# Batched 64x64 matmul on one core: the first tile of a loaded as fp32 by SyncE and ScalarE

## The chip, the cores and the metric

The kernel runs on one core of a Trainium2 chip. The metric is the device time of one execution in microseconds. The core has TensorE (PE, which also loads weights, shown as PEld), VectorE (DVE), ScalarE (ACT), GpSimd (POOL) and SyncE (SP), and sixteen DMA engines, which all queues share. SyncE, ScalarE and GpSimd can each issue DMAs on a queue of their own.

## The reference

```python
a = np.random.randn(1024, 64, 64).astype(np.float32)
b = np.random.randn(1024, 64, 64).astype(np.float32)
np.matmul(a, b).astype(np.float32)
```

1024 independent products of 64x64 matrices: 16.78 MB of `a`, 16.78 MB of `b` and 16.78 MB of result.

## The kernel before

The work is cut into 16 tiles `t` of 64 products each. `b` is loaded by such tiles (`load_b`, 1.05 MB each); `a` is loaded by 8 double tiles `s` of 128 products (`load_a`, 2.1 MB of fp32 each), so that tiles 2s and 2s+1 use double tile s.

**Loads of a.** `load_a(s)` issues four DMAs from GpSimd, one for each quarter `h`, into a tile `a_sb`. They cast from fp32 to bf16 on the way, so they write half of what they read. `a_pool` holds three such tiles.

**Loads of b.** `load_b(t)` issues one DMA from SyncE, or from ScalarE for tiles 1, 4, 6 and 7. `b_pool` holds four tiles. The loads of tiles 0 and 1 carry a gate: they wait until the second quarter of the first tile of `a` has landed.

**Preparing a.** `regroup(s)` copies `a_sb` into `a_bf` with the four quarters interleaved; it is one VectorE copy, and for `s == 0` four, one for each quarter. `transpose(s, j)` runs eight TensorE transposes with an identity matrix, taking pairs of bf16 as one fp32, and ScalarE copies the result from PSUM into `at_sb`. `spread(t)` then makes four VectorE copies that put the quarters on the diagonal blocks of a block-diagonal tile `at_bd`. There are two `at_bd` tiles, used in turn; both are set to zero at the start, the first by VectorE, the second by GpSimd, and only the diagonal blocks are ever rewritten.

**Multiplying.** `cast(t)` makes bf16 of `b` on ScalarE. `multiply(t)` runs 64 matmuls (128x128 weights from `at_bd`, 64 columns of `b`) into two PSUM tiles `o_ps`. ScalarE empties the first half and VectorE the second, four copies each, into a result tile `o_sb`; `o_pool` holds six. `store(t)` sends `o_sb` to memory from GpSimd, one tile after it was made (`HOLD = 2`); the last two tiles are stored in smaller pieces.

**Order.** The kernel is written under a manual schedule: each engine runs its instructions in the order of the program text, so an engine that waits holds up all that stands behind it. Before the loop over `t` stand the loads of the first three tiles of `a` and four of `b`, `regroup(0)`, both transposes of tile 0, `spread(0)`, `cast(0)`, `regroup(1)` and half of the transposes of tile 1. In the loop, each turn does `spread(t + 1)` and `cast(t + 1)`, the load of tile t+4 of `b`, on even turns `regroup(s + 2)` and the load of tile s+4 of `a`, then `multiply(t)`, half a set of transposes, and the store of the tile before. So VectorE empties tile 0 only after `regroup(2)`, that is after the third tile of `a` has landed. Every DMA from GpSimd signals on one of eight slots used in turn, and waits until the DMA that used its slot before has landed.

At the very start stand 100 small matmuls on zeros, which keep TensorE active before the first real work.

Of the kernel before, what the change touches and what calls it, by code (L numbers as in the profile page):

```python
# [8 lines left out]
fp32 = mybir.dt.float32  # L9
bf16 = mybir.dt.bfloat16  # L10
# [3 lines left out]
def kernel(  # L14
# [14 lines left out]
    nc = tc.nc  # L29
    B, M, K = a.shape  # L30
    _, _, N = b.shape
# [8 lines left out]
    a_v = a.rearrange("(s g h) (mp v) k -> s h g mp (v k)", h=4, g=32, v=16)  # L40
    b_v = b.rearrange("(t g h) (kp u) n -> t (h kp) g (u n)", h=4, g=16, u=2)
    o_v = out.rearrange("(t gh x) (mo w) n -> t (x mo) gh (w n)", gh=8, x=8, w=4)

    consts = ctx.enter_context(tc.tile_pool(name="consts", bufs=1))
# [3 lines left out]
    o_pool = ctx.enter_context(tc.tile_pool(name="o_pool", bufs=6))  # L48
    t_psum = ctx.enter_context(
        tc.tile_pool(name="t_psum", bufs=4, space=bass.MemoryType.PSUM)  # L50
    )
# [4 lines left out]
    bd_tiles = [  # L56
        consts.tile([128, 2, 16, 2, 4, 16], fp32, name=f"at_bd{i}") for i in range(N_BD)
    ]
    identity = consts.tile([128, 128], fp32)
    warm = consts.tile([128, 2], fp32)  # L60
    zeros = consts.tile([128, 32], bf16)
    a_tiles, b_tiles, abf_tiles, at_tiles, bbf_tiles = {}, {}, {}, {}, {}
    held, first_a = {}, []

    def load_a(s):
        a_sb = a_pool.tile([128, 4, 16, 64], bf16, name="a_sb")
        for h in range(4):
            load = nc.gpsimd.dma_start(  # L68
                out=a_sb[:, h, :, :].rearrange("p v k -> p (v k)"), in_=a_v[s, h]
            )  # L70
            if s == 0:
                first_a.append(load)
        a_tiles[s] = a_sb

    def load_b(t):
        b_sb = b_pool.tile([128, 16, 128], fp32, name="b_sb")
        queue = nc.scalar if t in (1, 4, 6, 7) else nc.sync
        load = queue.dma_start(out=b_sb[:], in_=b_v[t])  # L78
        if t < 2:
            tc.add_manual_dep(  # L80
                load.ins,
                first_a[1].ins.name,
                mybir.DependencyInfo(
                    mybir.DependencyClass.Sync, mybir.DependencyReason.DATA
                ),
                reason="first tile of a goes ahead",
            )
        b_tiles[t] = b_sb

    def regroup(s):  # L90
        a_sb = a_tiles.pop(s)
        a_bf = work.tile([128, 16, 4, 64], bf16, name="a_bf")

        for lo, hi in [(0, 1), (1, 2), (2, 3), (3, 4)] if s == 0 else [(0, 4)]:
            nc.vector.tensor_copy(  # L95
                a_bf[:, :, lo:hi, :],
                a_sb[:, lo:hi, :, :].rearrange("p h v k -> p v h k"),
            )
        abf_tiles[s] = a_bf
        at_tiles[s] = work.tile([128, 2, 32, 2, 4, 4], fp32, name="at_sb")  # L100

    def transpose(s, j):
        a_cols = abf_tiles[s][:].rearrange("p v h k -> p v (h k)").bitcast(fp32)
        for wl in range(2):
            at_ps = t_psum.tile([128, 4, 128], fp32, name="at_ps")
            for vo in range(4):
                nc.tensor.transpose(  # L107
                    at_ps[:, vo, :], a_cols[:, 4 * vo + 2 * j + wl, :], identity[:]
                )
            nc.scalar.copy(  # L110
                at_tiles[s][:, j, :, wl, :, :],
                at_ps[:].rearrange("p vo (g mp) -> p g mp vo", mp=4),
            )

    def spread(t):
        half = slice(16 * (t % 2), 16 * (t % 2) + 16)
        bd = bd_tiles[t % N_BD]
        for h in range(4):
            rows = slice(32 * h, 32 * h + 32)
            nc.vector.tensor_copy(  # L120
                bd[rows, :, :, :, h, :].rearrange("p j g wl mo -> p j (g wl) mo"),
                at_tiles[t // 2][rows, :, half, :, :, :].rearrange(
                    "p j g wl mp vo -> p j (g wl) (mp vo)"
                ),
            )

    def cast(t):
        b_bf = work.tile([128, 16, 128], bf16, name="b_bf")
        b_sb = b_tiles.pop(t)
        if t < n_t - 1:  # L130
            nc.scalar.copy(b_bf[:], b_sb[:])  # L131
        else:
            for gq in range(4):
                rows = slice(4 * gq, 4 * gq + 4)
                if gq % 2:
                    nc.vector.tensor_copy(b_bf[:, rows, :], b_sb[:, rows, :])
                else:
                    nc.scalar.copy(b_bf[:, rows, :], b_sb[:, rows, :])  # L138
        bbf_tiles[t] = b_bf

    def store(t):
        for piece in held.pop(t):
            piece()
# [49 lines left out]
            held[t] = [lambda q=q: put(q, 8 if whole else 4) for q in ([0] if whole else [0, 4])]  # L193

    with tc.manual_schedule():
        load_a(0)

        warm_ps = t_psum.tile([128, 4, 128], fp32, name="at_ps")
        nc.vector.memset(zeros[:], 0.0)
        for _ in range(100):  # L200
            nc.tensor.matmul(  # L201
                warm_ps[0:32, 0, 0:32], zeros[:], zeros[:], start=True, stop=True
            )

        nc.vector.memset(warm[:, 0:1], 0.0)  # L205
        nc.scalar.copy(warm[:, 1:2], warm[:, 0:1])  # L206
        for t in range(B_AHEAD):
            load_b(t)
        nc.vector.memset(bd_tiles[0][:], 0.0)  # L209
        make_identity(nc, identity)  # L210
        for s in range(1, A_AHEAD):
            load_a(s)
        nc.gpsimd.memset(bd_tiles[1][:], 0.0)  # L213
        regroup(0)
        transpose(0, 0)
        transpose(0, 1)
        spread(0)
        cast(0)
        regroup(1)
        load_a(A_AHEAD)  # L220
        transpose(1, 0)
        for t in range(n_t):
            s, half = t // 2, t % 2
            if t + 1 < n_t:
                spread(t + 1)
                cast(t + 1)
            if t + B_AHEAD < n_t:
                load_b(t + B_AHEAD)
            if half == 0:
                if s + 2 < n_s:  # L230
                    regroup(s + 2)
                if s + 1 + A_AHEAD < n_s:
                    load_a(s + 1 + A_AHEAD)
            multiply(t)
            if half == 0 and s + 1 < n_s:
                transpose(s + 1, 1)
            if half == 1 and s + 2 < n_s:
                transpose(s + 2, 0)
            if t >= HOLD - 1:
                store(t - HOLD + 1)  # L240
        for t in range(n_t - HOLD + 1, n_t):
            store(t)
# [30 lines left out]
```

## Time and profile before

| What | Value |
|---|---|
| Median of 9 runs | 135.89 us (135.55 to 136.08) |
| The profiled execution | 135.76 us, span 133.7 us |
| VectorE busy | 105.7 us, 79% of the span |
| ScalarE busy | 84.6 us, 63% |
| TensorE busy | 70.0 us, 52% |
| GpSimd busy | 44.4 us, 33% |
| HBM traffic | 33.55 MB read, 16.78 MB written |
| GpSimd's DMA queue | 25.17 MB written, 66.4% of the DMA engines' time |
| SyncE's DMA queue | 12.58 MB, 26.2% |
| ScalarE's DMA queue | 4.19 MB, 8.3% |

The span runs from the first to the last instruction in the profile; 2.06 us of the profiled execution lie outside it. Times below are microseconds from the start of the span. The DMA figures count written bytes, so a casting load of `a` shows half of the bytes that it reads. L68, for example, is line 68 of the kernel before: L68 is the issue of a load of `a`, L78 that of a load of `b`, L95 `regroup`, L107 and L110 the transposes and their copies, L120 `spread`, L131 to L138 `cast`, L153 the stores, L164 the emptying of PSUM, L176 the matmuls, L201 the matmuls on zeros, L209 and L213 the two memsets of `at_bd`.

### The profile page before, as it was taken

To read this page: it belongs to the slowest core of one execution; us is meant where nothing else is said; L and a number is where in the kernel's file an instruction comes from. 1 tells how busy PE (TensorE), PEld (TensorE's weight loads), DVE (VectorE), ACT (ScalarE), POOL (GpSimd) and SP (SyncE) were. 2 spreads that over 40 slices of the span, in tenths; PEclk is the share of its full clock that TensorE was granted. 3 is DMA by queue.
4 is the path that set the end of the run, shared out by engine and by line. 5 is a ranking of instruction groups with operands and counts; after the bars stand their busy time and mean duration, and the time that the engine had idled before them with its cause. 6 is when DMAs were issued, how large, how long until landed. Compare 5 with 4: busy or idle time off the path is not lost.

```text
span 133.7 us, 3019 instructions
## 1 busy us (share of the span) xinstructions
PE 70.0 (52%) x1252; PEld 65.7 (49%) x1252; DVE 105.7 (79%) x148; ACT 84.6 (63%) x123; POOL 44.4 (33%) x59
## 2 busy tenths in 40 slices
PE   7108205753991396439926963496349633668000
PEld 7008105743991395439915952485248522658000
DVE  5621559059899899998999999999999999999900
ACT  4003303996637999956699999659948939259300
POOL 6938634331512431225023251124031204042820
PEclk9955955586589658975797799769986998555955
DMA  2999999999999999999999999999999999999990
GB/s 13 189 200 259 307 306 287 273 283 310 307 278 274 352 361 284 302 332 389 393 338 267 289 390 392 317 269 300 398 396 393 395 398 395 394 404 406 385 347 34
DMA packets 17485, 42.14 MB, mean 315 GB/s; under 512 B 1088, under 2 KB 1088, under 8 KB 17472
## 3 DMA queue, kind: packets, MB, share of 16 engines
q0 software_dynamic: 9024, 25.17, 66.4%
q1 hardware_dynamic: 6336, 12.58, 26.2%
q10 hardware_dynamic: 2112, 4.19, 8.3%
q8 instruction: 10, 0.16, 0.5%
q14 instruction: 3, 0.02, 0.0%
HBM read 33.55 MB, written 16.78 MB: 376 GB/s over the span
## 4 chain that ended last, share of the span: by engine, by line
DMA 64%; DVE 14%; issue 12%; POOL 4%; POOLq 1%; DVEq 0%
DMA a_sb<-in_a_dram 50%; DMA out_dram<-o_sb 14%; DVE o_sb L164 8%; DVE at_bd L120 6%; POOL out_dram L153 3%; POOL a_sb L68 1%; POOLq L268 1%; DVE a_bf L95 0%; DVEq L95 0%; POOLq L153 0%; DVEq L120 0%; POOLq L257 0%
## 5 line engine op out<-in xcount | busy, mean ns | idle before, releaser
L176 PEld LDWEIGHTS <-at_bd 128*128 128x128 bf16 x1024 | 43.8, 114 | 42.7 <-DVE o_sb L164 25.5
L176 PE MATMUL o_ps<-b_bf,at_bd 128*128 128x64 bf16 x960 | 42.7, 215 | 37.7 <-DVE o_sb L164 23.4
L120 DVE COPY at_bd<-at_sb 32x1024 f32<-32x1024 f32 x64 | 46.5, 727 | 6.7 <-ACT at_sb L110 4.8
L164 DVE COPY o_sb<-o_ps 64x512 f32<-64x512 f32 x60 | 41.3, 688 | 2.1 <-PE o_ps L176 1.2
L164 ACT COPY o_sb<-o_ps 64x512 f32<-64x512 f32 x60 | 34.8, 580 | 6.8 <-PE o_ps L176 4.5
L131 ACT CAST b_bf<-b_sb 128x2048 bf16<-128x2048 f32 x15 | 28.6, 1905 | 13.8 <-DMA b_sb<-in_b_dram 13.8
L153 POOL DMA_DIRECT2D out_dram<-o_sb x20 | 20.1, 1005 | 48.7 <-DVE o_sb L164 17.1
L68 POOL DMA_DIRECT2D a_sb<-in_a_dram x32 | 20.3, 640 | 34.4 <-DMA a_sb<-in_a_dram 23.3
L107 PE MATMUL at_ps<-identity,a_bf 128*128 128x128 f32 x128 | 24.2, 354 | 13.4 <-DVE a_bf L95 13.4
L107 PEld LDWEIGHTS at_ps<-identity,a_bf 128*128 128x128 f32 x128 | 20.2, 187 | 13.7 <-issue 13.7
L110 ACT COPY at_sb<-at_ps 128x512 f32<-128x512 f32 x32 | 17.9, 588 | 10.3 <-PE at_ps L107 10.0
L95 DVE COPY a_bf<-a_sb 128x4096 bf16<-128x4096 bf16 (+1 forms) x11 | 10.3, 937 | 10.5 <-DMA a_sb<-in_a_dram 10.4
L176 PE MATMUL at_ps<-b_bf,at_bd 128*128 128x64 bf16 x64 | 3.5, 240 | 1.2 <-DVE at_bd L120 1.2
L209 DVE MEMSET at_bd<- 128x4096 f32 x1 | 3.5, 3472 | 0.8 <-issue 0.8
L213 POOL MEMSET at_bd<- 128x4096 f32 x1 | 3.5, 3530 | 0.0
L164 DVE COPY o_sb<-at_ps 64x256 f32<-64x256 f32 x8 | 3.4, 422 | 0.1
L138 ACT CAST b_bf<-b_sb 128x512 bf16<-128x512 f32 x2 | 1.1, 614 | 3.6 <-DMA b_sb<-in_b_dram 3.6
L201 PE MATMUL at_ps<-zeros 128*32 128x32 bf16 x100 | 2.8, 188 | 0.9 <-DVE warm L205 0.9
L201 PEld LDWEIGHTS <-zeros 128*32 128x32 bf16 x100 | 2.7, 103 | 0.9 <-DVE warm L205 0.9
L78 ACT MOVE_SHAPE b_sb<-in_b_dram x4 | 0.1, 24 | 4.8 <-DMA a_sb<-in_a_dram 4.8
L164 ACT COPY o_sb<-at_ps 64x256 f32<-64x256 f32 x8 | 2.9, 367 | 0.1
L206 ACT ACT_TABLE_LOAD x1 | 1.3, 1283 | 0.7 <-PEq L257 0.7
(10 smaller groups left out, 2.0 us busy)
## 6 DMA issues: line engine op xcount, KB each, us to landing
out_dram<-o_sb POOLq DMA_DIRECT2D x14, 1024.0 KB, 22.8
a_sb<-in_a_dram POOLq DMA_DIRECT2D x32, 256.0 KB, 18.5
out_dram<-o_sb POOLq DMA_DIRECT2D x2, 512.0 KB, 6.1
out_dram<-o_sb POOLq DMA_DIRECT2D x4, 256.0 KB, 5.5
b_sb<-in_b_dram SPq DMA_DIRECT2D x12, 0.5 KB, 21.7
b_sb<-in_b_dram ACTq DMA_DIRECT2D x4, 0.5 KB, 15.8
```

Of the source, the lines that this page charges most:

```text
L68: load = nc.gpsimd.dma_start(out=a_sb[:, h, :, :].rearrange("p v k -> p (v k)"), in_=a_v[s, h])
L95: nc.vector.tensor_copy(a_bf[:, :, lo:hi, :], a_sb[:, lo:hi, :, :].rearrange("p h v k -> p v h k"),)
L107: nc.tensor.transpose(at_ps[:, vo, :], a_cols[:, 4 * vo + 2 * j + wl, :], identity[:])
L110: nc.scalar.copy(at_tiles[s][:, j, :, wl, :, :], at_ps[:].rearrange("p vo (g mp) -> p g mp vo", mp=4),)
L120: nc.vector.tensor_copy(bd[rows, :, :, :, h, :].rearrange("p j g wl mo -> p j (g wl) mo"), at_tiles[t // 2][rows, :, half, :, :, :].rearrange(
L131: nc.scalar.copy(b_bf[:], b_sb[:])
L153: nc.gpsimd.dma_start(out=o_v[t, :, lo : lo + n, :], in_=o_sb[:, lo : lo + n].rearrange("p gh j wl n -> p (gh j wl n)"),)
L164: copy(dst, src)
L176: nc.tensor.matmul(o_ps[:, gl, g % 2, j, :], at_bd[:, j, g, :, u], b_bf[:, g, 64 * u : 64 * u + 64], start=(u == 0), stop=(u == 1),)
L201: nc.tensor.matmul(warm_ps[0:32, 0, 0:32], zeros[:], zeros[:], start=True, stop=True)
L209: nc.vector.memset(bd_tiles[0][:], 0.0)
L213: nc.gpsimd.memset(bd_tiles[1][:], 0.0)
```

## The change

Four things change, all in the opening of the kernel.

1. The first tile of `a` is loaded without a cast: quarters 0 and 2 by SyncE and 1 and 3 by ScalarE, as fp32, into two result buffers of `o_pool` that no result uses yet. These are the first instructions of both queues.
2. `regroup(0)` makes bf16 of the quarters while it interleaves them, quarters 0 and 2 on VectorE, 1 and 3 on ScalarE.
3. The loads of `b` lose their gate. They follow on the same queues, behind the quarters of `a`.
4. The 100 matmuls on zeros and the memset for them are gone. GpSimd, which has no load of tile 0 to issue, makes the identity matrix, zeroes the second `at_bd`, and then issues the loads of tiles 1 and 2 of `a`; before, this memset came after them.

```diff
+    def load_first_a():
+        raw = [
+            o_pool.tile([128, 8, 2, 2, 64], fp32, name="o_sb")[:].rearrange(
+                "p gh j wl n -> p (gh j wl n)"
+            )
+            for _ in range(2)
+        ]
+        parts = [raw[h % 2][:, 1024 * (h // 2) : 1024 * (h // 2) + 1024] for h in range(4)]
+        for h in range(4):
+            (nc.scalar if h % 2 else nc.sync).dma_start(out=parts[h], in_=a_v[0, h])
+        a_tiles[0] = parts
...
-        load = queue.dma_start(out=b_sb[:], in_=b_v[t])
-        if t < 2:
-            tc.add_manual_dep(
-                load.ins,
-                first_a[1].ins.name,
...
-                reason="first tile of a goes ahead",
-            )
+        queue.dma_start(out=b_sb[:], in_=b_v[t])
...
-        for lo, hi in [(0, 1), (1, 2), (2, 3), (3, 4)] if s == 0 else [(0, 4)]:
-            nc.vector.tensor_copy(
-                a_bf[:, :, lo:hi, :],
-                a_sb[:, lo:hi, :, :].rearrange("p h v k -> p v h k"),
-            )
+        if s == 0:
+            for h in range(4):
+                copy = nc.scalar.copy if h % 2 else nc.vector.tensor_copy
+                copy(a_bf[:, :, h, :], a_sb[h].rearrange("p (v k) -> p v k", v=16))
+        else:
+            nc.vector.tensor_copy(a_bf[:], a_sb[:].rearrange("p h v k -> p v h k"))
...
-        load_a(0)
-
-        warm_ps = t_psum.tile([128, 4, 128], fp32, name="at_ps")
-        nc.vector.memset(zeros[:], 0.0)
-        for _ in range(100):
-            nc.tensor.matmul(
-                warm_ps[0:32, 0, 0:32], zeros[:], zeros[:], start=True, stop=True
-            )
+        load_first_a()
...
         make_identity(nc, identity)
+        nc.gpsimd.memset(bd_tiles[1][:], 0.0)
         for s in range(1, A_AHEAD):
             load_a(s)
-        nc.gpsimd.memset(bd_tiles[1][:], 0.0)
         regroup(0)
```

## The prediction

> **What bounds the kernel now.** The first thing to read is the head of the page: the span, the DMA row of the slices, and the HBM traffic.
>
> ```profile
> span 133.7 us, 3019 instructions
> DVE  5621559059899899998999999999999999999900
> DMA  2999999999999999999999999999999999999990
> HBM read 33.55 MB, written 16.78 MB: 376 GB/s over the span
> ```
>
> The 16 DMA engines are busy from the second slice to the last but one, and VectorE (DVE) is nearly full from the tenth slice on. Two resources look like the bound, so the next question is which of them ends last. The DMA rate answers it. The GB/s column counts written bytes, and a load that casts `a` to bf16 reads twice what it writes. So I take the long middle stretch as one window, and five short ones at the start. Columns: busy us of PE, PEld, DVE, ACT, POOL with counts, then clock, DMA share, GB/s.
>
> ```profile
> 4.00:127.00 123.00, 67.15 (x1152) 63.00 (x1152) 103.36 (x146) 83.14 (x121) 40.88 (x49) 0.76 1.06 331
> 2.00:3.00 1.00, 1.00 (x45) 1.00 (x41) 1.00 (x1) 0.21 (x2) 1.00 (x2) 1.00 0.56 31
> 3.00:4.00 1.00, 0.77 (x30) 0.67 (x26) 1.00 (x1) 0.00 (x0) 0.93 (x4) 1.00 0.71 90
> 4.00:5.00 1.00, 0.00 (x0) 0.00 (x0) 1.00 (x1) 0.00 (x0) 1.00 (x3) 1.00 1.05 186
> 5.00:6.00 1.00, 0.00 (x0) 0.00 (x0) 0.47 (x2) 0.00 (x0) 1.00 (x3) 1.00 1.12 211
> ```
>
> From 4 to 127 us: 331 GB/s x 123 us = 40.7 MB written, and nearly all of the 8.4 MB that the casting loads read beyond what they write, so 49 MB in 123 us, or 0.398 MB per us. At 5 to 6 us, with only casting loads in flight, it is 2 x 211 KB, 0.42. The rate is nearly the same with loads of `a` alone, with a mix, and with stores alone (about 400 GB/s at 118 to 125 us). So the engines run at one ceiling from 4 us on, and the end is set by volume: 50.33 MB / 0.398 = 126.5 us after the moment at which they effectively start. That moment: 31 + 90 KB written by 4.0 us, 0.24 MB read, worth 0.6 us, so 4.0 - 0.6 = 3.4 us. 3.4 + 126.5 = 129.9 us; the last packet ends at 131.8 because the small last stores run slower (360 GB/s and less after 125 us) and the engines do not end together. The closing work takes the span to 133.7, and 2.06 us lie outside it (135.76 for the profiled execution; the median of the runs, 135.89, is 0.13 higher).
>
> Next, the waits and the timeline, to see how much the compute engines may slip.
>
> ```profile
> 1.28 2.32 POOL L68 DMA_DIRECT2D a_sb<-in_a_dram  x4 [0.84 <-POOLq L257]
> 1.72 3.47 DVE L209 MEMSET at_bd<- 128x4096 f32 x1 [0.82 <-issue]
> 7.04 23.28 SPq L78 DMA_DIRECT2D b_sb<-in_b_dram  x4
> 28.16 1.23 DVE L95 COPY a_bf<-a_sb 128x4096 bf16<-128x4096 bf16 x1 [4.88 <-DMA a_sb<-in_a_dram]
> 94.67 1.23 DVE L95 COPY a_bf<-a_sb 128x4096 bf16<-128x4096 bf16 x1 [0.26 <-DMA a_sb<-in_a_dram]
> 123.32 3.48 DVE L164 COPY o_sb<-at_ps 64x256 f32<-64x256 f32 x8
> 127.10 0.72 POOL L153 DMA_DIRECT2D out_dram<-o_sb  x1 [0.34 <-DVE o_sb L164]
> ```
>
> VectorE idles 4.88 us until the third tile of `a` has landed (28.16), then runs full until 94.67, where it again meets the DMA, then full to 126.80. The last store is issued at 127.10 and written out at 127.82; the stores before it land only at 130.3. So the last store queues for 2.5 us, and VectorE's whole chain could end some 2 us later before the end moves. Both chains are close, but DMA volume is the outer one.
>
> **The change part by part.** *Bytes.* `a` is read once as fp32 either way, and 2.1 MB of the first tile are written as fp32 where they were written as bf16. The ceiling goes by bytes read: a 4 KB casting packet takes 173 ns in the packet records, a 4 KB store packet 165 to 169. For 512 packets over 16 engines that is at most 32 x 8 ns = 0.26 us of gain; I take zero.
>
> *Start.* This is the term that counts. Before, GpSimd issues the first load at 1.28; the first packet is at 2.67, and 0.7 us more go in the ramp (3.4 - 2.67), because the four loads are issued one each 0.58 us and the first packets take up to 1.1 us. Afterwards SyncE and ScalarE issue two loads each as soon as they are free, about 0.75 (ScalarE's first own instruction starts at 0.73), with all four queued by about 2.2 (ScalarE's issues of `b` take 0.7 to 0.84 each). The unknown is the time from such an issue to its first packet. Nearest rows: `b`, same queues, issued at 7.04, first packet at 11.28 (4.24 us; ScalarE's later ones 4.2 and 4.3), but with the engines full and 2,048 runs of 512 B to describe; and `a` on GpSimd, engines idle, 128 runs of 4 KB, 0.8 us after the 0.58 us of issuing. The new loads have the shape and the idle engines of the second and the queue of the first. I take 1.7 us, nearer the second. First packet at 2.45, 0.4 us of ramp: effective start 2.85, against 3.4: gain 0.55 us. With 0.8 us and 0.3 of ramp it is 1.85, gain 1.55; with 4.24 us and 0.5 of ramp 5.5, loss 2.1.
>
> The Trainium skill, "DMA: Bandwidth & Descriptors", section "Latency and other measured facts", gives about 0.6 us to the first byte on this path against about 1 us on GpSimd's. This case's rows say otherwise for `b` (4.24 us) and 1.39 us from issue for `a`. By the page the start would be 0.75 + 0.6 + 0.4 = 1.75 us and the gain 1.65.
>
> *GpSimd.* It loses four issues at the start (2.32 us) and makes identity and the 3.53 us memset of the second `at_bd` first; both are from rows (0.27 + 0.29 us). Its first load is then issued at about 5.4, or about 9 if the memset has to wait for VectorE's, which now runs beside it (no row shows the two together). The tile of `a` that was issued from 4.13 on is 1.3 to 5 us later. That leaves the DMA engines no gap: tile 0 and four tiles of `b`, 6.3 MB or 16 us, are queued by then. If `b` alone ran for up to 2 us at 84 to 96 ns per 2 KB packet (about 364 GB/s), it would lose 0.2 us; I take zero, against the packet term above. Four loads fewer on the same eight completion slots also means that the next eight need wait for no earlier landing.
>
> The Trainium skill, "SBUF — State Buffer", section on the "DVE blocks DMA" trap, says that VectorE in a two-port mode keeps GpSimd from writing descriptors, and that loads from SyncE or ScalarE escape this. The rows show no such stall here: four issues in 2.32 us lie inside VectorE's memset (1.72 to 5.19). By the page the move would free those issues; by the rows it frees nothing beyond the start.
>
> *The gates on b.* Before, the first tiles of `b` were issued at 7.04; now behind tile 0 on the same queues. The first lands at about 18 instead of 21.7 us. The bytes are the same and the engines were full of `a` meanwhile, so this is worth nothing at the end; it only makes multiply(0) earlier, and VectorE stands behind the third tile of `a` anyway.
>
> *Regroup of tile 0.* Removed: four VectorE copies of 0.43. Added: two VectorE casts of 128x1024, by the 128x512 cast (L136, 0.38 each) 0.76 each, and two ScalarE casts of 0.95 (half of L131's 1.905). The last piece is ready some 0.5 us later after landing, but it lands near 8.5 instead of 10. Covered by the 4.88 us before 28.16; without that cover 0.5 us.
>
> *Warm-up.* One hundred matmuls, 2.84 us on an idle TensorE, end at 3.78. The tile-0 transposes start at 10.65 with the granted clock at 0.62 and take 3.47 for 16. At half clock later groups of 8 take 1.95, so losing any warm-up costs at most 0.4 us, again under the 4.88.
>
> *Result buffers.* Two of six `o_sb` hold raw `a` until about 9 us; the fifth and sixth result tiles want them only after 50 us. Free.
>
> Sum: 135.76 - 0.55 = 135.2; on the median of the runs, 135.3 us. Less than 0.2% (0.27 us) can't be told from no change.
>
> **The rivals.** *Slower: the new queue wakes late.* If the first load needs the 4.2 us of the `b` rows, the engines stand idle until about 5 and nothing covers it, since GpSimd's loads come at 5.4 or after. Price 2.1 us: 137.9 to 138.0. It decides from 2.24 us on (0.75 + 2.24 + 0.4 = 3.4). For it: three rows agree; against: all three come under load and with 16 times the runs. At 3 us it would be 136.7.
>
> *Nothing.* The first packet comes at 2.7 to 3.0, the ramp is no steeper than before: 135.7 to 136.1. For it: the slow first packets (up to 1.1 us) may belong to the memory and not the queue.
>
> *More.* The issue takes 0.8 us or the page's figure, and the last stores find a longer backlog and lose less than the 1.9 us they lose now: 133.9 to 134.5. Against: the last packets are slower because each store is small.
>
> *Slower through VectorE*: the third tile of `a` lands over 2 us later than 28.16 because its loads are issued late. By volume it can't: in 28 us the engines move 9.8 MB whatever the order, and it needs 6.3 of them with `b` taking its share. 136.5 if so.
>
> **How the numbers follow.** Forecast (gain 0.3 to 1.4) 0.46; nothing 0.17; late queue 0.21; more 0.10; VectorE 0.06. Range 134.2 to 137.0: it cuts off most of "more" (0.08) and the half of the late queue that lies above 137.0 (0.10). The forecast's own range is 134.5 to 135.6. Faster by over 0.2% (below 135.62) are forecast and more, 0.56; within 0.2% nothing, 0.17; slower the late queue and VectorE, 0.27.
>
> **What would show it.** In the profile after: GB/s in the windows from 2 to 4 us well above 31 and 90 (the new tile writes all that it reads, so 400 is full); the last store landing earlier by as much; the DMA row full from the second slice on; VectorE's wait for the third tile still there. A DMA row that stays empty until 5 us, or a gap in it near 8 us before GpSimd's loads come, would make the prediction wrong; so would a last store that lands right after its own issue, since VectorE would then be the bound.

## The result, and the profile after

The kernel after the change takes 135.22 us (median of 9 runs, 135.03 to 135.44) against 135.81 (29 runs of the kernel before). The ratio is 0.9954, with an interval of 0.9945 to 0.9963: 0.6 us faster. The profiled execution took 135.24 us, with a span of 133.5.

The head of the page, answering to the lines of before:

```profile
span 133.5 us, 2820 instructions
DVE  5720438249899989997999999999799999999930
DMA  3999999999999999999999999999999999999892
HBM read 33.55 MB, written 16.78 MB: 377 GB/s over the span
```

The DMA engines are full from the second slice to the third last. Then come an 8, a 9 and a 2, where before it was 9, 9 and 0, and VectorE now reaches into the last slice but one. So something was gained at the start and part of it given back at the end. The windows show both (columns as before: busy us of the five engines, clock, DMA share, GB/s written):

```profile
2.00:3.00 1.00, 0.00 (x0) 0.00 (x0) 1.00 (x1) 0.69 (x2) 1.00 (x1) 1.00 0.95 135
3.00:4.00 1.00, 0.00 (x0) 0.00 (x0) 1.00 (x1) 0.79 (x2) 1.00 (x1) 1.00 0.82 270
4.00:5.00 1.00, 0.00 (x0) 0.00 (x0) 1.00 (x1) 0.00 (x0) 1.00 (x2) 1.00 1.03 381
...
124.00:127.00 3.00, 0.45 (x9) 0.29 (x6) 2.88 (x7) 1.10 (x4) 1.98 (x3) 0.50 0.84 306
```

By 4.0 us 135 + 270 = 405 KB have moved, and a plain load writes what it reads. Before it was 0.24 MB by the same windows. By the packet records, which give the start and the duration of every packet, with a packet under way at 4.0 us counted by its share, it is 0.38 MB against 0.21. At 0.398 MB per us both ways of counting give some 0.4 us. In the last window of this fence the engines run at 306 GB/s. The kernel before, in the same stretch and the one ahead of it:

```profile
118.00:124.00 6.00, 4.03 (x74) 3.75 (x71) 5.82 (x10) 5.55 (x12) 1.64 (x3) 0.58 1.02 404
124.00:127.00 3.00, 0.00 (x0) 0.00 (x0) 2.71 (x7) 0.84 (x3) 2.46 (x4) 0.91 1.02 384
```

The timeline of the kernel after names both ends:

```profile
0.73 1.55 ACTq L82 DMA_DIRECT2D o_sb<-in_a_dram  x2
0.74 1.27 SPq L82 DMA_DIRECT2D o_sb<-in_a_dram  x2
1.25 3.51 POOL L205 MEMSET at_bd<- 128x4096 f32 x1
1.69 3.47 DVE L203 MEMSET at_bd<- 128x4096 f32 x1 [0.83 <-issue]
4.70 5.11 POOL L67 DMA_DIRECT2D a_sb<-in_a_dram  x8
28.53 1.23 DVE L99 COPY a_bf<-a_sb 128x4096 bf16<-128x4096 bf16 x1 [4.15 <-DMA a_sb<-in_a_dram]
95.73 1.23 DVE L99 COPY a_bf<-a_sb 128x4096 bf16<-128x4096 bf16 x1 [0.89 <-DMA a_sb<-in_a_dram]
124.45 3.48 DVE L165 COPY o_sb<-at_ps 64x256 f32<-64x256 f32 x8
128.23 0.72 POOL L154 DMA_DIRECT2D out_dram<-o_sb  x1 [0.34 <-DVE o_sb L165]
```

The loads of tile 0 are issued at 0.73 and 0.74 instead of 1.28, and their first packet comes at 2.15 instead of 2.67. But GpSimd's loads, behind its memset, begin at 4.70 and not at 1.28. VectorE gets the third tile of `a` at 28.53 (before 28.16), the last one at 95.73 (94.67), and ends at 127.93 (126.80). The last store is issued 1.13 us later than before, and the last packet ends at 131.57 instead of 131.78.

The median span of the timed runs fell from 133.8 us (runs of the kernel before, made beside the experiments) to 133.35. What lies outside the span fell from about 1.95 to 1.75. So some 0.45 us of the gain are in the span and 0.2 outside it. In the two profiled executions it is divided otherwise: 0.2 us in the span and 0.3 outside, of 0.52.

### The profile page after: what moved, and what is told of

The parts are those of the page before. It is cut to its first block, busy times and chain, and to the rows that moved or that the text cites. A ratio compares the mean times of both kernels' runs of the same rounds, so it can differ in the third digit from the quotient of the medians.

```text
span 133.5 us, 2820 instructions
## 1 busy us (share of the span) xinstructions
PE 68.5 (51%) x1152; PEld 64.4 (48%) x1152; DVE 105.3 (79%) x145; ACT 86.6 (65%) x125; POOL 43.7 (33%) x55
## 4 chain that ended last, share of the span: by engine, by line
DMA 61%; DVE 14%; issue 12%; POOL 9%; POOLq 1%; DVEq 0%
DMA a_sb<-in_a_dram 46%; DMA out_dram<-o_sb 15%; DVE o_sb L165 8%; DVE at_bd L121 6%; POOL out_dram L154 3%; POOL a_sb L67 3%; POOL at_bd L205 3%; POOLq L262 1%; POOL identity masks.py:199 0%; DVE a_bf L99 0%; POOL identity masks.py:197 0%; POOLq L154 0%; DVEq L99 0%; POOLq masks.py:199 0%; DVEq L121 0%
## 5 line engine op out<-in xcount | busy, mean ns | idle before, releaser
L177 PEld LDWEIGHTS <-at_bd 128*128 128x128 bf16 x1024 | 45.1, 116 | 41.4 <-DVE o_sb L165 26.9
L177 PE MATMUL o_ps<-b_bf,at_bd 128*128 128x64 bf16 x960 | 44.1, 218 | 36.5 <-DVE o_sb L165 24.9
L67 POOL DMA_DIRECT2D a_sb<-in_a_dram x28 | 19.3, 700 | 37.8 <-DMA a_sb<-in_a_dram 27.2
L99 DVE COPY a_bf<-a_sb 128x4096 bf16<-128x4096 bf16 x7 | 8.6, 1228 | 7.7 <-DMA a_sb<-in_a_dram 7.6
L97 ACT CAST a_bf<-o_sb 128x1024 bf16<-128x1024 f32 x2 | 2.1, 1044 | 4.7 <-DMA o_sb<-in_a_dram 4.7
L97 DVE CAST a_bf<-o_sb 128x1024 bf16<-128x1024 f32 x2 | 1.5, 735 | 3.1 <-DMA o_sb<-in_a_dram 2.9
L137 DVE CAST b_bf<-b_sb 128x512 bf16<-128x512 f32 x2 | 0.8, 426 | 0.0
```

The source lines that it names most:

```text
L67: nc.gpsimd.dma_start(out=a_sb[:, h, :, :].rearrange("p v k -> p (v k)"), in_=a_v[s, h])
L97: copy(a_bf[:, :, h, :], a_sb[h].rearrange("p (v k) -> p v k", v=16))
L99: nc.vector.tensor_copy(a_bf[:], a_sb[:].rearrange("p h v k -> p v h k"))
L177: nc.tensor.matmul(o_ps[:, gl, g % 2, j, :], at_bd[:, j, g, :, u], b_bf[:, g, 64 * u : 64 * u + 64], start=(u == 0), stop=(u == 1),)
```

## The experiments

Theory: the end is set by how many bytes the DMA engines have moved early, that is, by when they start and whether they stay full; VectorE's chain has some slack. Rivals: the gates, the order on GpSimd or the warm-up carry the gain; or VectorE's chain is the real bound.

**One part of the change at a time, on the kernel before.** The warm-up alone:

```diff
-        nc.vector.memset(zeros[:], 0.0)
-        for _ in range(100):
-            nc.tensor.matmul(...)
```

> The kernel before, without the 100 matmuls on zeros and their memset. Theory (the gain comes from the DMA engines' earlier start): the loads start as before, 135.8 us, ratio within 0.1% of 1, span 133.7 and 2.06 us outside it. Rival (part of the gain lies outside the span, because the program is 200 TensorE instructions shorter; after the change 1.75 us lie outside it): about 0.3 us faster, 135.5, with the span unchanged and 1.75 us outside. Second rival (TensorE stays at half clock without the warm-up and the chain gets later): 0.1 to 0.4 us slower, the span longer.

Measured: 135.70 us, ratio 0.9994 (0.9979 to 1.0008): no change. Outside the span it has 1.88 us where the kernel before has 1.97 in the same job, so at most 0.1 us lies there. Its other direction, on the kernel after:

```diff
         load_first_a()
+        nc.vector.memset(zeros[:], 0.0)
+        for _ in range(100):
+            nc.tensor.matmul(...)
```

> The kernel after the change, with the 100 matmuls on zeros put back. Theory: 135.2 us as without them, ratio to before 0.995. Rival (shorter program): 135.5 us, ratio 0.998, with 2.06 us outside the span. If the matmuls cost nothing outside the span, the 0.3 us between the two kernels there come from something else.

Measured: 135.44 us, ratio 0.9983 (0.9970 to 0.9996), 1.86 us outside the span. That is 0.2 us above the kernel after, 0.1 of it outside the span. The theory expected nothing. With the pair before it, shortening TensorE's program takes about 0.1 us outside the span. What the matmuls cost inside it is not settled: the median span is the same in the first pair (133.8) and 0.25 us longer here (133.6 against 133.35).

The route of the first tile alone (the new load function and casts; gates, warm-up and GpSimd's order stay):

```diff
-        load_a(0)
+        load_first_a()
```

> The kernel before, with one thing changed: the first tile of a goes as fp32 by SyncE and ScalarE into result buffers and is cast in regroup(0); the gates on b, the warm-up and the order on GpSimd stay. Theory: first packet near 2.2 us, 0.18 MB more moved by 4 us than before, so 0.4 to 0.5 us faster in the stretch up to 28 us; GpSimd's loads of the second tile come at about 1.4 us now and keep the engines full behind the gate, so 135.2 to 135.4. Rival (the gates and the order matter): less than 0.2 us of gain.

Measured: 135.15 us, ratio 0.9963 (0.9950 to 0.9977). This part by itself gives the whole gain. Two groups of its timeline are worth a look:

```profile
5.11 4.91 DVE L111 CAST a_bf<-o_sb 128x1024 bf16<-128x1024 f32 x1
11.21 0.69 DVE L111 CAST a_bf<-o_sb 128x1024 bf16<-128x1024 f32 x1 [1.18 <-DMA o_sb<-in_a_dram]
5.82 3.65 POOL L228 MEMSET at_bd<- 128x4096 f32 x1
126.64 0.72 POOL L168 DMA_DIRECT2D out_dram<-o_sb  x1 [0.34 <-DVE o_sb L179]
```

VectorE's first cast takes 4.91 us where the second, of the same shape, takes 0.69. It ends at 10.02, half a microsecond after GpSimd's memset ends at 9.47. This stall is covered by VectorE's wait for the third tile, and the last store is even issued earlier than before, at 126.64.

The gates alone (the condition and its dependency in `load_b` taken out):

```diff
-        if t < 2:
-            tc.add_manual_dep(load.ins, first_a[1].ins.name, ...)
```

> The kernel before, with only the gates on b taken away. The bytes that start the engines are now those of b: issued near 0.75 us, first packet near 2.2 us (b has 2,048 short runs, so perhaps later, up to 4.2 us after the issue, when it would change nothing at the start). Theory (only the start of the engines counts, not what is loaded first): faster by up to 0.4 us if b's first packet comes at 2.2, no change if it comes after 2.7. Rival (the tile of a on the path): the first tile of a lands about 4 us later (14 us) as it shares with b, the third tile about as before, time within 0.2 us or slower by up to 0.5 us.

Measured: 136.74 us, ratio 1.0069 (1.0047 to 1.0092), 0.9 us slower. The DMA engines did start earlier: by 28 us they had moved 9.99 MB, against 9.84 before. But by the packets that signal completion tile 0 has landed only at 17.2 instead of 9.7 us, and the chain behind it is late to the end:

```profile
118.00:124.00 6.00, 3.37 (x60) 3.22 (x61) 5.80 (x9) 3.64 (x8) 2.54 (x2) 0.50 0.93 356
124.00:127.00 3.00, 2.11 (x40) 1.95 (x37) 2.92 (x6) 2.54 (x7) 0.56 (x1) 0.50 0.85 287
129.97 0.72 POOL L144 DMA_DIRECT2D out_dram<-o_sb  x1 [0.34 <-DVE o_sb L155]
```

At 118 to 124 us the engines are down to 356 GB/s (404 before): the stores have run out. The last store comes 2.87 us later than before. So "only the start of the engines counts" falls: past its slack VectorE's chain sets the end.

**The start as a dose.** The kernel after, with the loads of tile 0 held back until ScalarE's first copy is done (the function makes each load depend on the instruction that it is given):

```diff
-        load_first_a()
-
         nc.vector.memset(warm[:, 0:1], 0.0)
-        nc.scalar.copy(warm[:, 1:2], warm[:, 0:1])
+        load_first_a(nc.scalar.copy(warm[:, 1:2], warm[:, 0:1]))
```

> The kernel after the change, with the loads of the first tile of a held until ScalarE's first copy is done (about 2.2 us instead of 0.73), and all of b behind them; GpSimd is left alone. First packet at about 3.7 us instead of 2.15. Theory (each microsecond of later start is a microsecond at the end): 1.3 to 1.6 us slower than the kernel after, 136.5 to 136.8. Rival (compute sets the end, the start has 1 to 2 us of slack): less than 0.5 us slower, below 135.7.

```profile
2.00:3.00 1.00, 0.00 (x0) 0.00 (x0) 1.00 (x1) 0.21 (x2) 1.00 (x1) 1.00 0.00 0
3.00:4.00 1.00, 0.00 (x0) 0.00 (x0) 1.00 (x1) 0.18 (x1) 1.00 (x1) 1.00 0.35 70
```

Measured: 136.34 us, ratio 1.0050 (1.0035 to 1.0064), 1.1 us above the kernel after. The first packet comes 1.5 us later (3.67), and by 28 us 0.50 MB fewer have moved, which at 0.398 MB per us is 1.25 us. The last packet ends 1.09 us later. So the loss is nearly one to one with the bytes; it falls short of the expected 1.3 to 1.6 because the engines catch up a part: 1.5 us at full rate would be 0.60 MB, 0.54 are missing by 8 us and 0.50 by 28. VectorE's last store comes 1.23 us later as well, so this run shows that a late start is paid for, not which of the two chains carries the delay to the end.

**The order on GpSimd, and VectorE's chain.** The kernel after, with the second memset behind the loads again:

```diff
-        nc.gpsimd.memset(bd_tiles[1][:], 0.0)
         for s in range(1, A_AHEAD):
             load_a(s)
+        nc.gpsimd.memset(bd_tiles[1][:], 0.0)
```

> The kernel after the change, with GpSimd's memset of the second at_bd put back behind the loads of the second and third tile of a, as before the change. GpSimd then issues its first load at about 1.3 us instead of 4.7. Theory (with the start gained, the end is set by how late VectorE's chain gets the third and the last tile of a): the third tile lands at 27.5 to 28.0 instead of 28.4, the last store is issued at 126.7 to 127.5 instead of 128.23, the end comes 0.1 to 0.3 us earlier: 134.9 to 135.1. Rival (volume alone counts): the start is the same, so is the time, 135.2.

```profile
1.47 4.48 POOL L67 DMA_DIRECT2D a_sb<-in_a_dram  x8 [0.16 <-issue]
127.31 0.72 POOL L154 DMA_DIRECT2D out_dram<-o_sb  x1 [0.33 <-DVE o_sb L165]
```

Measured: 134.83 us, ratio 0.9936 (0.9922 to 0.9950), 0.4 us better than the change as made and the fastest kernel here. The moved memset was a cost inside the change. Two things came together, and this run doesn't part them. GpSimd's first packets arrive at 5.28 instead of 8.56, and 10.12 MB have moved by 28 us instead of 10.00, worth 0.3 us; and the last store is issued 0.92 us earlier.

The same with the second memset on VectorE, behind `regroup(0)`:

```diff
-        nc.gpsimd.memset(bd_tiles[1][:], 0.0)
         regroup(0)
+        nc.vector.memset(bd_tiles[1][:], 0.0)
```

> The kernel after the change with the second at_bd zeroed by VectorE, behind regroup(0), instead of by GpSimd ahead of its loads. GpSimd issues its first load at 1.47 us and never touches SBUF while VectorE casts. Theory on the port (VectorE's cast took 4.9 instead of 0.7 us where GpSimd's memset was running): the two casts take 0.7 each, the memset 3.5 in VectorE's idle time from 10 to 15 us. Theory on the time (volume from the start decides, and VectorE has slack before the third tile of a): as with the memset put back behind the loads, 134.8, within 0.15 us. Rival (the early chain matters): 0.2 to 0.5 us faster than that.

```profile
5.16 0.76 DVE L97 CAST a_bf<-o_sb 128x1024 bf16<-128x1024 f32 x1
```

Measured: 134.96 us, ratio 0.9937 (0.9923 to 0.9952), the same as with the memset last. The cast is back at 0.76 us although GpSimd issues loads beside it, so it was the memset that held it up. As expected the stall of 4 us cost nothing at the end. This run also helps to part the two things of the one before: it has moved 10.00 MB by 28 us, no more than the kernel after, and is still 0.26 us faster, with its last store issued 0.67 us earlier (127.56). So in this run more bytes early do not account for the gain.

The route alone and no gates (this kernel is also the one with the memset last, with the warm-up put back):

```diff
-        load_a(0)
+        load_first_a()
...
-        if t < 2:
-            tc.add_manual_dep(load.ins, first_a[1].ins.name, ...)
```

> The kernel before with the new route of the first tile (135.15 us), and without the gates on b; warm-up and GpSimd's order stay as before the change. Theory (behind tile 0 on the same queues the gates hold back nothing that the engines lack, and GpSimd's loads fill them anyway): 135.0 to 135.2, within 0.15 us of the gated one. Rival (without gates the engines are fuller between 4 and 9 us): 0.2 to 0.4 us faster, 134.8, as without the warm-up.

Measured: 135.13 us, ratio 0.9959 (0.9945 to 0.9973), the same as with the gates (135.15). Once tile 0 stands first on the queues that carry `b`, the gates are worth nothing. The 0.3 us between this kernel and the one without the warm-up (134.83) are like the 0.2 us that the warm-up cost the kernel after, and are only partly outside the span (1.90 against 1.79 us).

So the change can be followed part by part: 135.81 before, 135.15 with the route, 135.13 without the gates too, 134.83 without the warm-up too, and 135.22 with GpSimd's memset ahead of its loads, which is the kernel after.

**VectorE's end.** The last cast of `b` moved to ScalarE, on three kernels, which takes 0.77 us off VectorE's chain shortly before its end:

```diff
-                if gq % 2:
-                    nc.vector.tensor_copy(b_bf[:, rows, :], b_sb[:, rows, :])
-                else:
-                    nc.scalar.copy(b_bf[:, rows, :], b_sb[:, rows, :])
+                nc.scalar.copy(b_bf[:, rows, :], b_sb[:, rows, :])
```

On the kernel after:

> The kernel after the change, with the last tile of b cast by ScalarE alone, where VectorE did two of its four parts (0.77 us on VectorE, when ScalarE had 3.2 us to spare). Theory (in the kernel after the change the last stores run out of backlog, since VectorE's chain ends 1.1 us later than before): the last store is issued 0.7 us earlier, at about 127.5, and the end comes 0.2 to 0.5 us earlier: 134.7 to 135.0. Rival (the end is set by DMA volume alone): no change, 135.2.

Measured: 135.43 us, ratio 0.9968 (0.9956 to 0.9979): not faster. The last store was issued at 127.41 and the last packet ended at 131.17 instead of 131.57, but the median span (133.3) is that of the kernel after, and 2.12 us instead of 1.75 lie outside it. On the kernel before with the route alone:

> The kernel before with only the first tile's route changed, and the last cast on ScalarE alone. There the last store was issued at 126.64 and landed at 131.40, 4.8 us later, behind a full queue. Theory (volume decides where the queue is full): VectorE ends 0.7 us earlier and the time stays within 0.1 us of 135.15. Rival (VectorE's end decides in every kernel): 0.5 to 0.7 us faster, 134.5.

Measured: 135.18 us, ratio 0.9963 (0.9949 to 0.9977). The time stays, as the theory says. But the median span is 0.3 us shorter (133.0), about half of what the rival expected, and again 0.3 us more lie outside it (2.20). On the kernel before without the gates:

> The kernel before without the gates on b (136.7 us, span 134.8, last store issued at 129.97), with the last tile of b cast by ScalarE alone. Theory (in that kernel VectorE's chain, not the DMA volume, sets the end): the last store is issued 0.8 us earlier and the span falls by 0.6 to 0.9 us. Rival (its loss comes from slower or idle DMA engines, not from VectorE): the span falls by less than 0.2 us.

```profile
128.24 0.72 POOL L141 DMA_DIRECT2D out_dram<-o_sb  x1 [0.34 <-DVE o_sb L152]
```

Measured: 135.69 us, ratio 0.9994 (0.9969 to 1.0019). Here the move brings 1.05 us, and the median span falls by 0.95, from 134.8 to 133.85. The last store is issued 1.73 us earlier in the profiled execution. So in that kernel VectorE's chain was the bound, and in the other two the time shows no cost of it. How much it cost is less sure: the gain is larger than the 0.77 us that were taken off the chain, and the runs of both kernels spread widely (135.79 to 137.58 without the move, 134.88 to 136.49 with it).

**All kernels by one rule.** If volume decides, the last packet ends at 131.78 - (MB moved by 28 us - 9.84) / 0.398, with the kernel before as the reference. The MB are summed from the packet records, a casting load counted by what it reads:

| Kernel | Time, us | MB by 28 us | Last store issued | Last packet ends | By the rule |
|---|---|---|---|---|---|
| before | 135.81 | 9.84 | 127.10 | 131.78 | (reference) |
| before, no warm-up | 135.70 | 9.79 | 127.42 | 132.10 | 131.91 |
| before, no gates | 136.74 | 9.99 | 129.97 | 132.85 | 131.40 |
| before, no gates, last cast | 135.69 | 9.95 | 128.24 | 131.64 | 131.50 |
| route alone | 135.15 | 10.10 | 126.64 | 131.40 | 131.13 |
| route alone, last cast | 135.18 | 10.13 | 126.1 | 131.10 | 131.05 |
| route, no gates | 135.13 | 10.03 | 127.51 | 131.27 | 131.30 |
| after | 135.22 | 10.00 | 128.23 | 131.57 | 131.38 |
| after, warm-up | 135.44 | 9.92 | 128.41 | 131.67 | 131.58 |
| after, last cast | 135.43 | 10.08 | 127.41 | 131.17 | 131.18 |
| after, late start | 136.34 | 9.50 | 129.46 | 132.66 | 132.63 |
| after, memset last | 134.83 | 10.12 | 127.31 | 131.01 | 131.08 |
| after, both memsets on VectorE | 134.96 | 10.00 | 127.56 | 131.25 | 131.38 |

Eleven of the twelve lie within 0.3 us of the rule, which spans 131.05 to 132.63. The one that doesn't, 1.45 us off, is the one in which VectorE's chain came latest. The bytes and the ends are from one profiled execution of each kernel. How far such figures scatter shows in the last two rows: GpSimd's first loads are issued at 1.47 in both, and yet they differ by 0.12 MB, or 0.3 us. So the rule can't show effects below that.

The kernel after is 0.19 us off the rule, but a count near the end says more about what VectorE's later end costs it. By 124 us it has moved 48.11 MB against 47.89 before, a lead of 0.22 MB or 0.55 us, and its last packet ends only 0.21 us earlier. The run with both memsets on VectorE has the same lead at 124 us (0.23 MB), then runs at 337 GB/s where the kernel after has 306, and ends 0.32 us before it. By these executions the late end costs some 0.3 us; the median span, which did not fall when the last cast was moved (133.3 against 133.35), shows no such cost. It lies between nothing and 0.3 us.

## Why the prediction was right, point by point

The time was 135.22 us against 135.3 predicted, and by the mechanism that was put first: bytes moved early. That the sum came so close is partly luck, for the terms were less exact. In the runs the new route alone brings 0.66 us where 0.55 were predicted, leaving out the warm-up 0.3 more, and the memset ahead of GpSimd's loads takes 0.4 back; for the last two nothing had been counted. Three of the signs that were named came: the windows from 2 to 4 us, the full DMA row, and VectorE's wait for the third tile. A fourth, a last store that lands earlier by as much, did not: the last packet ended 0.21 us earlier, not 0.55.

**Start.** Predicted: issue at 0.75, first packet 1.7 us later at 2.45, 0.4 us of ramp. Measured: 0.74, 1.41 us later at 2.15, and by the windows the effective start is 4.0 - 0.405 / 0.398 = 2.98 instead of 2.85, so a ramp of 0.8 us. The latency was taken too long and the ramp too short. The packet records show two things in the ramp: first packets that take up to 1.47 us where 159 ns is usual later, and no packet of ScalarE's queue before 4.06, when SyncE's first quarter was through, although all four loads were issued by 2.3. How much each of them cost is not shown. The ramp also differs from one execution to the next: the kernels that started on time with the new route had moved 0.38 to 0.53 MB by 4.0 us. The gain at the start by the windows is 3.39 - 2.98 = 0.41 us, 0.55 predicted. By the packet records it is 0.44 at 4 us and 0.52 at 8, and 0.40 at 28 us.

The rival of the late queue did not happen; the 4.2 us of the loads of `b` are not what 128 long runs on idle engines need. The Trainium skill, "DMA: Bandwidth & Descriptors", section "Latency and other measured facts", gives about 0.6 us to the first byte; 1.41 us were measured from the start of SyncE's issue, which itself took about 0.6.

**Bytes.** Taken as nothing, and so it was. The plain packets were shorter than the casting ones (159 ns against 173), but from 5 to 8 us both kernels moved 1.26 MB: 426 + 418 + 420 KB after, and twice 211 + 219 + 201 KB before.

**GpSimd.** The memset took 3.51 us and did not wait for VectorE's (3.47, side by side), so the loads started at 4.70, better than the 5.4 of the prediction. The engines had no gap, as forecast. What was missed is that these loads are worth having early: with GpSimd's first one at 1.47 the kernel is 0.3 to 0.4 us faster (134.96 and 134.83). The prediction priced this reordering at zero; it is the term that was mis-sized most. Whether the loss comes by fewer bytes early or by VectorE's later end is not settled, as said above.

**Slack of VectorE.** Predicted: some 2 us before the end moves, and no more than a third tile that comes as before. The slip was missed, the slack nearly right. In the kernel after VectorE ended 1.13 us later, as the third tile came 0.37 and the last one 1.06 us later, and this cost between nothing and 0.3 us. Without the gates the last store was 2.87 us late and the end 1.45 us behind the rule, so 1.4 us were free, from an end that the earlier start had itself brought forward by 0.4. The last store took 2.9 us from issue to last packet there, against 4.7 before: that is the queue that can be used up. The 2.5 us of queue in the prediction rest on a misread row: 130.3 is the landing of a store issued at 124.33. The store just ahead of the last one, issued at 126.06, took 5.5 us and landed near 131.6.

**Gates.** Worth nothing as they were removed here, as predicted, but only because tile 0 stands ahead on the same queues; removed alone they cost 0.9 us. The first tile of `b` landed at 18.6 by its completion packets (18 predicted).

**Regroup and warm-up.** Casts of 0.74 and 1.04 us against 0.76 and 0.95; the 16 transposes took 3.65 us against 3.47. Both were hidden: VectorE still waits 4.15 us for the third tile.

**Not predicted:** the 0.2 us outside the span. About half of it goes with the 100 matmuls; the other half stays open, as do the extra 0.3 us outside the span that moving the last cast to ScalarE brought on two kernels and not on the third.

**The port.** The prediction held a row against a rule of the skill, and chose the wrong row. The Trainium skill, "SBUF — State Buffer", section "Who interferes with whom", says that VectorE's copies and casts in a two-port mode and a GpSimd operation exclude each other, the one issued first holding the port for its whole instruction; of a VectorE memset it says so for trn3 alone. So the row with VectorE's memset was no test of it, and the gain that the prediction derived from the page does not follow from it. Other rows of before were:

```profile
19.30 1.23 DVE L95 COPY a_bf<-a_sb 128x4096 bf16<-128x4096 bf16 x1 [1.58 <-DMA a_sb<-in_a_dram]
19.46 1.18 POOL L68 DMA_DIRECT2D a_sb<-in_a_dram  x1 [2.25 <-DMA a_sb<-in_a_dram]
24.22 0.53 POOL L68 DMA_DIRECT2D a_sb<-in_a_dram  x1 [0.81 <-DMA a_sb<-in_a_dram]
28.32 1.18 POOL L68 DMA_DIRECT2D a_sb<-in_a_dram  x1 [1.52 <-DMA a_sb<-in_a_dram]
```

An issue on GpSimd that begins while VectorE copies 128x4096 (from 19.30 and, as the prediction shows, from 28.16) takes 1.18 us and ends 0.11 us after the copy; with VectorE idle it takes 0.53. So the stall that the prediction did not find is in the kernel before, 0.65 us each time; for the issues of tile 0, which run beside a memset, its reading stands. The runs with a cast beside GpSimd's memset show the other direction: 4.91 us against 0.69. There the cast begins by the profile 0.7 us ahead of the memset and yet is the one that waits, so the order that the skill names is not shown. In the kernel after, GpSimd's memset stands out of the cast's way and runs beside a memset, at full speed on both.

## What to carry to other kernels

Where the DMA engines are full from start to end, a kernel ends when its volume is through, and an opening is worth what it adds to the bytes moved in the first microseconds: count them, with a casting load taken by what it reads. Put the data that the chain needs first at the head of the queue, and let every queue start at once: a memset of 3.5 us ahead of GpSimd's first load cost 0.3 to 0.4 us here, although the engines had no gap. Check how long the last store waits for its turn, and distrust that wait as slack: what stands in front of it may be as late as it is.

## What the runs showed of the hardware

- Two queues filled at the same time did not share the engines at first. In each kernel with the new route ScalarE's first packet came within 0.01 us of the first completion of SyncE's quarter (4.06 in the kernel after, 3.78 to 3.86 in the others that started on time, 5.27 with the late start). So it looks as if each engine took its eight 4 KB packets (128 over 16 engines) from one queue before it turned to the other; the records do not name the engine. The Trainium skill, "DMA: Bandwidth & Descriptors", section "Queues, rings and completion order", says that an engine drains a whole packet of some 9 to 17 descriptors from one queue before it switches. Eight and the completion fit that, if what the trace calls a packet is one descriptor, which no run here shows.
- The time from issue to first packet of a load of `b` was 4.2 to 4.6 us on full engines, and 1.6 us for SyncE's first one on idle engines in the kernel without gates (issued at 0.80, first packet at 2.38). So the rival's rows were slow by the load on the engines, not by the number of 512-byte runs in the load.
- A plain 4 KB load packet took 159 ns where a casting one took 172 to 173.
- A VectorE cast of 0.69 us stretched to 4.8 to 4.9 us in all four kernels where GpSimd's memset of 3.65 us ran beside it, and to no more than 0.8 where it did not.
